# Seven-product down units: one VectorE take replaced by a ScalarE copy and an accumulating DMA, and a one-column sigmoid behind the samples' softmax

## The chip, the cores and the metric

The kernel runs on one core of a Trainium2 chip. The metric is device time in microseconds (us) of one execution, the median of several runs. The engines are TensorE (PE; its weight loads are PEld), VectorE (DVE), ScalarE (ACT), GpSimd (POOL) and SyncE (SP); each works through its own queue in order, and semaphores order them against each other. SP issues the loads of weights, POOL the accumulating DMAs.

## The reference

One inference step of a hybrid encoder trunk of two layers (model width 1024). It works on 640 frames at once: 512 of a new stream and 16 each of eight running streams. Each layer is, cut to its core:

```
x += 0.5 * swiglu(rmsnorm(x, norm_ffn1), w_ffn1_gu, w_ffn1_down)      # "a0", "a1"
z  = rmsnorm(x, norm_mix) @ w_in            # conv B, C, V | q, k, v | gates
y_c = B * causal_depthwise_conv3(C * V)
y_a = chunk_band_attention(q, k, v, rel_bias)   # 8 heads x 64
m  = sigmoid(g_c) * (y_c @ w_conv_out) + sigmoid(g_a) * (y_a @ w_attn_out)
x += m @ w_o
x += 0.5 * swiglu(rmsnorm(x, norm_ffn2), w_ffn2_gu, w_ffn2_down)      # "b0", "b1"

def swiglu(h, w_gu, w_down):                # w_gu: 1024 x 5632, w_down: 2816 x 1024
    g, u = split(h @ w_gu, 2)
    return (silu(g) * u) @ w_down
```

A final RMSNorm follows. New keys, values and conv rows are outputs too. All data are float32.

## The kernel before

**Layout.** `x` is held transposed in SBUF: `xall` has 128 partitions, 8 rows of the model width and 640 columns, the frames. `t1` and `t2` are the columns 0 to 319 and 320 to 639. Each product is done in three matmuls of float32r, with both operands split into a high and a low part (`whi`, `wlo` for weights): high by high, low by high, high by low. ScalarE makes the high parts with a copy (`ACT.copy`, L307 for weights), VectorE the low parts with a subtraction (L312).

**Seven products for eight.** Most of the big products treat their operands as 2 x 2 blocks and use a scheme of seven block products in place of eight. The operand combinations are named X11, X21, XN6, XT5, XT7, X22 and XT4; the weights of one unit are four slabs, each a sum or a plain piece. One PSUM bank collects several of these products in turn, and in between it is read out, with what it holds at that moment: later products add to it.

**The feed-forward networks.** `ffn` goes over 22 units of 128 of the 2816 hidden channels, in chunks (`FFNS`): a0 4, 4, 4, 4, 4, 2; b0 2, 4, 4, 4, 8; a1 4, 4, 4, 4, 4, 2; b1 3, 4, 4, 4, 4, 3. `gate_up` does the gate and up products of one unit by seven. A chunk of four that is neither before the plain part nor the last is also multiplied with `w_down` by seven: `down_rows`, twice for each chunk (a first call for the rows of `x` 0 to 3, and a second, `second = True`, for 4 to 7), called during the next chunk behind its second and third `gate_up` units. That makes 4, 3, 5 and 4 chunks in a0, b0, a1 and b1. The last chunk goes into `x` by plain products and takes the next norm's inputs with it (`nxt.final`).

**One `down_rows` call.** Banks A (two halves, tile names `daa`, `dab`) and B (`dba`, `dbb`) and two single banks `c` (`dca`, `dcb`) are filled by TensorE in this order, twelve matmuls each (L960): X11 into A, X21 into B, XN6 on top of A, XT5 into `c`, XT7 on top of A, X22 on top of `c`, XT4 on top of A. What a bank holds after a step goes into `x` in one of two ways. `take` (L989) is one VectorE instruction that reads the bank and adds it, scaled, to the rows of `x`. `stage` (L974, L977) is a ScalarE copy of the bank into an SBUF tile of the tag `cap`, which has five buffers in turn, and `send` (L984) an accumulating DMA from there into `x`, issued by POOL. `c1_` (A after X11), `u2_` (A after XN6) and `c5_` (`c` after XT5) go by stage and send; B, `c` after X22, and A after XT7 and after XT4 by take. The next product that adds to a bank must wait until it has been read.

`gate_up` uses the same `cap` buffers: one for `c1_`/`u2` (named `both` in the code) and one for `c5_`.

**Order.** Under `manual_schedule` the named engines work in the order of the program. In the first two units that feed a chunk by seven this holds for TensorE, VectorE and ScalarE; after that (`free`) only TensorE's order is fixed, and a scheduler sets the others', up to the last chunk.

**The mixer.** `attention` fixes only TensorE's order. It does the prompt's attention and then that of the eight samples: `sscores(b)` (scores and `softmax`, whose exponential is L1604 and reciprocal L1607) and `svalues(b)`. Between them the stream `others` runs, whose last piece is the first pair of gates, `gate_pair(0)`, with the layer's first two sigmoids (L1125). Then comes `outputs`, in program order on three engines: its first `gate_pair` (banks `qa`, `qb`, `qc`) copies the bank `qa` with ScalarE at L1277 after X11 and at L1287 after XN6. ScalarE evaluates a function from a table of its set; going to a function of another set takes an ACT_TABLE_LOAD. The tile `early` (one column) is written by activations that serve only to bring a table in.

Of the kernel before, what the change touches and what calls it, by code (L numbers as in the profile page):

```python
# [12 lines left out]
AF = mybir.ActivationFunctionType  # L13
# [7 lines left out]
NB = 8  # L21
# [10 lines left out]
FT = FF // P  # L32
# [150 lines left out]
def trunk(ctx: ExitStack, tc: tile.TileContext, xin, wst, small, pbias, samplebias, kcache, vcache,  # L183
# [44 lines left out]
    for kind, inside in kinds():  # L228
        n = len(fourth)
# [118 lines left out]
    class Tiles:  # L348
# [6 lines left out]
        def take(self):  # L355
            if self.at == self.n:
                self.cur, (kind, _, width) = slab(hold[0])
                assert kind == "plain"
                self.at, self.n = 0, width // P
            j = self.at  # L360
            self.at += 1
            return tuple(c[:, j * P : (j + 1) * P] for c in self.cur)
# [578 lines left out]
                next(p.work)  # L941
                p.done += 1

    def down_rows(fp, n, ms, pairs, tails, later):


        A, B = (acc(f"d{i}{n}") for i in "ab")
        a, b = ([z[:, u, :HT] for u in range(2)] for z in (A, B))
        c = [att(f"dc{n}_{u}")[:, :HT] for u in range(2)]
        t1, t2 = slice(0, HT), slice(HT, T)  # L950
        second = ms[0] > 0

        def mul(ps, s, half, kind, start):
            for u in range(2):
                for i, pair in enumerate(pairs):
                    kp = half * NP + 2 * u + i
                    wh, wl = (z[:, kp * P : (kp + 1) * P] for z in s)
                    xh, xl = pair.X[kind]
                    for j, (w, y) in enumerate(((wh, xh), (wh, xl), (wl, xh))):
                        PE.matmul(ps[u], w, y, start=start and i == 0 and j == 0,  # L960
                                  stop=i == 1 and j == 2, skip_group_check=True)

        def place(name):
            step(later, f"r{int(second)}{name}")

        def tail():
            for t in tails:
                t(False)
            tails.clear()

        def stage(name, ps, scale=0.5):
            z = fp.tile([P, 2, HT], F32, tag="cap", name=f"{name}{n}", bufs=5)
            if ps is A:
                ACT.activation(z, two(A), AF.Copy, scale=scale)  # L974
            else:
                for u in range(2):
                    ACT.activation(z[:, u], ps[u], AF.Copy, scale=scale)  # L977
            return z

        def rows(r, cols):  # L980
            return xall[:, ms[r] : ms[r] + 3 : 2, cols]

        def send(z, r, cols):
            POOL.dma_start(rows(r, cols), z, accum_op=ALU.add)  # L984

        def take(ps, r, cols, scale=0.5):
            xs = rows(r, cols)
            for d, z in ((xs, two(ps)),) if ps in (A, B) else zip((xs[:, 0], xs[:, 1]), ps):
                DVE.scalar_tensor_tensor(out=d, in0=z, scalar=scale, in1=d, op0=ALU.mult, op1=ALU.add)  # L989

        s0 = quiet()
        mul(a, s0, 0, X11, True)
        c1 = stage("c1_", A)
        prep(used[0] + 1)
        begin()
        if not second:
            tail()
        flush()
        place("d1")
        mul(b, s0, 1, X21, True)  # L1000
        take(B, 0, t1)
        send(c1, 0, t1)
        s1 = slab(True)[0]
        flush()
        mul(a, s1, 0, XN6, False)
        u2 = stage("u2_", A)
        mul(c, s1, 1, XT5, True)
        c5 = stage("c5_", c, -0.5)
        s2 = slab(True)[0]
        if second:  # L1010
            tail()
        mul(a, s2, 0, XT7, False)
        take(A, 1, t2, -0.5)
        send(c5, 1, t2)
        flush()
        ahead()
        mul(c, s2, 1, X22, False)
        take(c, 0, t2)
        send(u2, 0, t2)
        s3 = slab(True)[0]  # L1020
        ahead()
        mul(a, s3, 0, XT4, False)
        take(A, 1, t1, -0.5)
        flush()

    def ffn(name, fp, ex, goff, after, end=False):


        act, tails, later, pairs = {}, [], [], {}
        first_two = FFNS[name][0][-1] == 4  # L1030
        nxt = None
        chunks, plain = FFNS[name]
        last = FT - chunks[-1]
        hold[0] = True

        mode = ExitStack()
        free = min(j for j in range(FT) if by_seven(name, j)) + 2

        def order(engines):
            mode.close()  # L1040
            mode.enter_context(tc.manual_schedule(engines=engines))

        order(ORDERED)
        if plain:
            ex = opening(fp, name, goff, plain, act.__setitem__, tails)
        for what, a in ffn_order(name):
            if what == "gu" and a == free:
                order({mybir.EngineType.PE})
            if what == "cut":
                order(ORDERED)  # L1050
            if what in ("std", "cut"):
                continue
            if what == "gu":
                pair = None
                if by_seven(name, a):
                    i, odd = divmod(a - chunk_at(name, a)[0], 2)
                    if not odd:
                        at = chunk_at(name, a)[0]
                        rows = at and by_seven(name, at - 1)
                        pairs[a] = Pair(fp, f"{name}_{a}", i, later, TURNS[i if rows else i + 2])  # L1060
                    pair = pairs[a - odd]
                gate_up(fp, f"{name}_{a}", ex, a == plain, tails, act.__setitem__, a, pair, later,
                        a - chunk_at(name, a)[0])
                continue
            if what == "rows":
                ms, js = a
                down_rows(fp, f"{name}_{js[0]}_{ms[0]}", ms, [pairs[j] for j in js[::2]], tails, later)
                continue
            js = a[0][1]
            if js[0] == last or len(a) * len(js) >= KT:  # L1070
                for t in tails:
                    t()()
                tails.clear()
            if after is not None and js[0] == last:
                nxt = nxt or after()
            if end and js[0] == last:
                nxt.all([act[j] for j in js])
                break
            for m, js in a:
                if js[0] == last and m < 2 and first_two:  # L1080

                    if m == 0:
                        two_pd = [acc(f"pd{name}_{js[0]}_{i}") for i in range(2)]
                        ws = [[tiles.take() for _ in js] for i in range(2)]
                        for ks in (js[:-1], js[-1:]):
                            for p, w in zip(two_pd, ws):
                                for j in ks:
                                    multiply(p, w[j - js[0]], act[j], j == js[0], j == js[-1])
                    pd = two_pd[m]
                else:  # L1090
                    pd = acc(f"pd{name}_{js[0]}_{m}")
                    product(pd, [act[j] for j in js])
                done = nxt and m == KT - 1
                if nxt:
                    nxt.weights(m)
                DVE.scalar_tensor_tensor(out=halves(x[m]), in0=two(pd), scalar=0.5,
                                         in1=halves(x[m]), op0=ALU.mult, op1=ALU.add)
                if not done:
                    flush()
                if nxt:  # L1100
                    nxt.final(m)
        hold[0] = False
        if not nxt:
            flush()
        mode.close()
        return nxt
# [240 lines left out]
    def attention(l, h, norms, stats, ops, mp, yas, ycp, both, others):  # L1347
# [170 lines left out]
        def sscores(b):  # L1518
# [22 lines left out]
            with soon():  # L1541
                DVE.tensor_tensor_reduce(out=s, in0=pss, in1=sbias, scale=1.0, scalar=NEG,
                                         op0=ALU.add, op1=ALU.max, accum_out=st[:, 0, 0:1])

                softmax(s, st, [(0, KS)])
            held[b] = box, st, vraw, vn

        def svalues(b):
# [48 lines left out]
    def softmax(s, st, parts):  # L1597


        n = len(parts)  # L1600
        with soon():
            DVE.tensor_scalar(out=st[:, 1, :n], in0=st[:, 0, :n], scalar1=-1.0, scalar2=None, op0=ALU.mult)
        for i, (o, w) in enumerate(parts):
            ACT.activation(s[:, o : o + w], s[:, o : o + w], AF.Exp, bias=st[:, 1, i : i + 1],  # L1604
                           accum_out=st[:, 2, i : i + 1])
        with soon():
            DVE.reciprocal(st[:, 3, :n], st[:, 2, :n])  # L1607
# [286 lines left out]
```

## Time and profile before

| | |
|---|---|
| time, median of 3 runs | 2521.71 us (2521.63 to 2521.96) |
| time of the profiled execution | 2522.08 us |
| its span, first to last instruction | 2520.3 us |
| TensorE busy | 2501.4 us |
| VectorE busy | 2118.3 us |
| ScalarE busy | 1325.6 us |
| POOL busy | 185.4 us |
| takes in `down_rows`, L989, 128x640 from bank A | 64, 0.82 us each |
| accumulating DMAs, L984 | 96 of 320 KB each |

In the rows of the profile, L12 is line 12 of the kernel; a name such as `daa` or `c_a` is the program's name of a tile without its numbers, the tile written stands before the arrow and those read behind it. "idle before ... <-" names what ended an engine's wait. Rows in the order of time begin with the start and the duration in us. A matmul's duration reaches into the next one's, so the distance of starts tells TensorE's pace.

### The profile page before, as it was taken

Reading aid. Unit: us, or ns where it says so; the run is one execution under the profiler, and the core shown is the slowest. Engines: PE = TensorE matmul, PEld = TensorE weight load, DVE = VectorE, ACT = ScalarE, POOL = GpSimd, SP = SyncE. Lnnn points to the kernel's source line nnn. Section 1 sums busy time; section 2 is a strip of 40 time slices with the busy share of each in tenths; the row PEclk is TensorE's granted clock in tenths of the full one; section 3 lists DMA queues with packets and bytes.
Section 4 is the critical chain, followed back from the end, with each engine's and each line's share of the span. In section 5 each row is a group of like instructions: output and inputs, shape, how many; then the busy total and the mean of one; then the engine's idle time right before and its main releaser. Section 6 shows DMA issues by size and latency. Waiting matters only on the chain.

```text
span 2520.3 us, 42929 instructions
## 1 busy us (share of the span) xinstructions
PE 2501.4 (99%) x17192; PEld 2440.7 (97%) x17192; DVE 2118.3 (84%) x3347; ACT 1325.6 (53%) x2084; POOL 185.4 (7%) x249
## 2 busy tenths in 40 slices
PE   9999999999999999999999999999999999999998
PEld 8999999888999999999999999998889999999998
DVE  7889888878677899988699999888786768899997
ACT  7445556664444545555455555557644455455553
POOL 0000112111000001000001000021110000010000
PEclk9999999999999999999999999999999999999999
DMA  4233444334222234343224343443342222243434
GB/s 144 76 104 104 115 115 126 107 113 163 76 84 93 76 101 115 105 111 100 84 76 113 111 116 100 115 118 124 130 138 84 76 93 76 86 114 109 123 100 99
DMA packets 99320, 265.40 MB, mean 105 GB/s; under 512 B 9680, under 2 KB 45136, under 8 KB 99120
## 3 DMA queue, kind: packets, MB, share of 16 engines
q1 hardware_dynamic: 69408, 220.76, 26.7%
q0 software_dynamic: 28992, 41.26, 9.3%
q8 instruction: 135, 2.21, 0.4%
q10 hardware_dynamic: 720, 0.65, 0.1%
q14 instruction: 65, 0.53, 0.1%
HBM read 222.70 MB, written 7.94 MB: 92 GB/s over the span
## 4 chain that ended last, share of the span: by engine, by line
PE 92%; DVE 4%; ACT 3%; issue 1%; DMA 0%; SPq 0%; DVEq 0%; ACTq 0%
PE pab L397 12%; PE paa L397 11%; PE pcb L397 6%; PE pca L397 5%; PE daa L960 5%; PE py L374 4%; PE po L374 4%; PE qa L397 4%; PE pdb L374 4%; PE dab L960 4%; PE pbb L397 3%; PE pba L397 3%; PE pda L374 2%; PE pv L1400 2%; PE ma_cv L397 2%; PE poa L374 2%
## 5 line engine op out<-in xcount | busy, mean ns | idle before, releaser
L312 DVE TENSOR_TENSOR wlo<-raw,whi 128x1024 fp32r<-128x1024 f32 (+1 forms) x566 | 586.4, 1039 | 177.7 <-ACT whi L307 173.3
L307 ACT CAST whi<-raw 128x1024 fp32r<-128x1024 f32 (+1 forms) x566 | 509.1, 903 | 371.4 <-PE pbb L397 38.7
L307 ACT CAST whi<-s 128x1024 fp32r<-128x1024 f32 (+1 forms) x152 | 144.4, 950 | 272.3 <-issue 89.2
L397 PE MATMUL pab<-xhib,whi 128*128 128x320 f32 x704 | 218.0, 310 | 0.0
L397 PE MATMUL pab<-xhib,wlo 128*128 128x320 f32 x704 | 217.6, 309 | 0.0
L397 PE MATMUL pab<-xlob,whi 128*128 128x320 f32 x704 | 217.4, 309 | 0.0
L397 PE MATMUL paa<-xhia,wlo 128*128 128x320 f32 x640 | 197.7, 309 | 0.7 <-DVE wlo L312 0.7
L397 PE MATMUL paa<-xhia,whi 128*128 128x320 f32 x640 | 197.9, 309 | 0.0
L397 PE MATMUL paa<-xloa,whi 128*128 128x320 f32 x640 | 197.5, 309 | 0.0
L312 DVE TENSOR_TENSOR wlo<-s,whi 128x1024 fp32r<-128x1024 f32 (+1 forms) x152 | 166.5, 1096 | 9.8 <-ACT whi L307 9.8
L397 PEld LDWEIGHTS pab<-xhib,wlo 128*128 128x128 f32 x704 | 132.1, 188 | 0.3
L397 PEld LDWEIGHTS pab<-xhib,whi 128*128 128x128 f32 x704 | 132.2, 188 | 0.2
L397 PEld LDWEIGHTS pab<-xlob,whi 128*128 128x128 f32 x704 | 132.2, 188 | 0.2
L397 PEld LDWEIGHTS paa<-xhia,wlo 128*128 128x128 f32 x640 | 120.1, 188 | 1.3 <-DVE wlo L312 1.3
L397 PEld LDWEIGHTS paa<-xhia,whi 128*128 128x128 f32 x640 | 120.1, 188 | 0.1
L397 PEld LDWEIGHTS paa<-xloa,whi 128*128 128x128 f32 x640 | 120.1, 188 | 0.1
L984 POOL DMA_DIRECT2D x<-c_b x28 | 33.8, 1208 | 1105.2 <-ACT c_b L977 457.5
L397 PE MATMUL pcb<-xhib,wlo 128*128 128x320 f32 x352 | 108.9, 309 | 0.0
L397 PE MATMUL pcb<-xhib,whi 128*128 128x320 f32 x352 | 108.7, 309 | 0.0
L397 PE MATMUL pcb<-xlob,whi 128*128 128x320 f32 x352 | 108.7, 309 | 0.0
L984 POOL DMA_DIRECT2D x<-c_a x36 | 43.6, 1211 | 865.0 <-ACT whi L307 386.2
L251 DVE TENSOR_TENSOR raw<-raw,raw 128x512 f32<-128x512 f32 x152 | 103.9, 684 | 1.1 <-DMA raw<-in_wst 0.5
(681 smaller groups left out, 7945.5 us busy)
## 6 DMA issues: line engine op xcount, KB each, us to landing
raw<-in_wst SPq DMA_DIRECT2D x378, 512.0 KB, 3.5
x<-c_a POOLq DMA_DIRECT2D x36, 320.0 KB, 4.1
x<-c_b POOLq DMA_DIRECT2D x28, 320.0 KB, 4.1
kc<-in_kcache SPq DMA_DIRECT2D x32, 256.0 KB, 3.9
vc<-in_vcache SPq DMA_DIRECT2D x16, 512.0 KB, 4.5
x<-u_a POOLq DMA_DIRECT2D x18, 320.0 KB, 5.4
x<-u_b POOLq DMA_DIRECT2D x14, 320.0 KB, 5.5
bias<-in_pbias POOLq DMA_DIRECT2D x16, 256.0 KB, 3.7
```

Of the source, the lines that this page charges most:

```text
L251: DVE.tensor_tensor(out=out, in0=a, in1=b, op=ALU.add)
L307: ACT.copy(hi[:, d], src[:, c])
L312: DVE.tensor_tensor(out=lo, in0=src, in1=hi.bitcast(F32), op=ALU.subtract)
L374: PE.matmul(ps[:, a, :HT], w, x[:, a * HT : (a + 1) * HT], start=first and j == 0, stop=last and j == 2)
L397: PE.matmul(ps, a, b, start=start and kp == 0 and j == 0, stop=stop and kp == NP - 1 and j == 2, skip_group_check=True)
L960: PE.matmul(ps[u], w, y, start=start and i == 0 and j == 0, stop=i == 1 and j == 2, skip_group_check=True)
L984: POOL.dma_start(rows(r, cols), z, accum_op=ALU.add)
L1400: PE.matmul(pv[t], xx[:, t * P : (t + 1) * P], w[:, kk * AW : (kk + 1) * AW], start=c == 0 and kk == 0 and j == 0, stop=c == KT // 2 - 1 a ...
```

## The change

`down_rows` gets a flag `border`. It is true for the last chunk by seven of a network if the chunk behind it has fewer than four units, which is so in a0, a1 and b1 and not in b0; 3 of 16 chunks, so 6 of 32 calls. Where it is false, A after XT7 no longer goes into `x` by the VectorE take: ScalarE copies it, scaled by -0.5, into a new `cap` tile `c7_`, and POOL adds it to the rows of `x` by DMA, ahead of the DMA of `c5_` into the same place. In the mixer, the last `sscores` gets a sigmoid of one column into `early`, which reads what the softmax's reciprocal wrote.

```
-    def down_rows(fp, n, ms, pairs, tails, later):
+    def down_rows(fp, n, ms, pairs, tails, later, border):
...
         mul(a, s2, 0, XT7, False)
-        take(A, 1, t2, -0.5)
+        if border:
+            take(A, 1, t2, -0.5)
+        else:
+            send(stage("c7_", A, -0.5), 1, t2)
         send(c5, 1, t2)
...
-                down_rows(fp, f"{name}_{js[0]}_{ms[0]}", ms, [pairs[j] for j in js[::2]], tails, later)
+                down_rows(fp, f"{name}_{js[0]}_{ms[0]}", ms, [pairs[j] for j in js[::2]], tails, later,
+                          js[-1] + 1 == last and FT - last < 4)
...
                 softmax(s, st, [(0, KS)])
+                if b == NB - 1:
+                    ACT.activation(early, st[:, 3, 0:1], AF.Sigmoid)
             held[b] = box, st, vraw, vn
```

## The prediction

> **What bounds the kernel now.** I read the page first: the busy shares and the chain of work that ended last.
>
> ```profile
> span 2520.3 us, 42929 instructions
> PE 2501.4 (99%) x17192; PEld 2440.7 (97%) x17192; DVE 2118.3 (84%) x3347; ACT 1325.6 (53%) x2084; POOL 185.4 (7%) x249
> PE 92%; DVE 4%; ACT 3%; issue 1%; DMA 0%; SPq 0%; DVEq 0%; ACTq 0%
> ```
>
> TensorE is busy for 2501.4 of 2520.3 us. The change alters none of its instructions, so it can only win back, or add to, the moments in which TensorE waits. VectorE's 84% is no bound by itself, and lightening it brings nothing except where VectorE is what TensorE waits for. So the second view is the list of waits, by the weight loads that precede each matmul (what waited, for whom, us in total, times, longest):
>
> ```profile
> PEld daa L960 <- DVE x L989: 2.8, 7, 0.4
> PEld dab L960 <- DVE x L989: 2.4, 6, 0.4
> PEld qa L397 <- ACT capsm L1287: 1.3, 2, 0.6
> ```
>
> Two of the entries belong to the places that the diff touches. Thirteen times a `down_rows` call waits 0.4 us (5.2 in all) for a VectorE take (L989), and twice the gate products of the mixer wait 0.6 us for a ScalarE copy. Thirteen is a number that the code knows: of the 16 chunks done by seven (4, 3, 5 and 4 in a0, b0, a1 and b1) three are the border chunks that keep the take, one each in a0, a1 and b1; 3 + 4 = 7 are left in the two a's (`daa`) and 3 + 3 = 6 in the two b's (`dab`). Each has two calls, so 26 calls change, and one of the two waits in each chunk. The third view, the order of time, shows which one. This is a second call (`ms[0] > 0`) of a0, TensorE's rows first:
>
> ```profile
> 202.57 0.31 PE L960 MATMUL daa<-thia,wlo 128*128 128x320 f32 x1
> ...
> 204.18 0.31 PE L960 MATMUL dca<-aloa,whi 128*128 128x320 f32 x1
> 204.33 0.31 PE L960 MATMUL dca<-ahia,wlo 128*128 128x320 f32 x1
> 204.77 0.42 PE L960 MATMUL daa<-t4hia,whi 128*128 128x320 f32 x1
> 205.03 0.31 PE L960 MATMUL daa<-t4loa,whi 128*128 128x320 f32 x1
> ```
>
> Matmuls start 0.15 us apart (204.18 to 204.33). The XT7 block ends with the one that starts at 202.57 and runs 0.31, at 202.88. Twelve matmuls into `c` follow, and XT4 adds to bank A again, due at 204.33 + 0.15 = 204.48. It starts at 204.77, and the next start comes 0.26 after instead of 0.15. The call loses (0.44 - 0.15) + (0.26 - 0.15) = 0.40 us; 13 x 0.40 = 5.2, the sum of the wait rows. What XT4 waits for is the reading of A, on VectorE:
>
> ```profile
> 202.76 1.23 DVE L312 TENSOR_TENSOR wlo<-raw,whi 128x1024 fp32r<-128x1024 f32 x1 [0.45 <-ACT whi L307]
> 203.90 0.82 DVE L989 SCALAR_TENSOR_TENSOR x<-daa,x 128x640 f32<-128x640 f32 x1
> ```
>
> The take could start at 202.88, but a weight subtraction of 1.23 us is ahead of it; it ends at 204.72, and XT4 starts 0.05 later. In a first call the take is in time:
>
> ```profile
> 178.63 0.82 DVE L989 SCALAR_TENSOR_TENSOR x<-daa,x 128x640 f32<-128x640 f32 x1
> 179.83 0.31 PE L960 MATMUL daa<-t4hia,whi 128*128 128x320 f32 x1
> ```
>
> It ends at 179.45, 0.38 before XT4 starts.
>
> **The third block on ScalarE.** What ScalarE does around the late call, and the time that a copy of the same size out of the same bank takes there (min/median/max ns):
>
> ```profile
> 202.62 0.73 ACT L924 CAST thia<-doa 128x640 fp32r<-128x640 f32 x1
> 204.58 1.05 ACT L307 CAST whi<-s 128x1024 fp32r<-128x1024 f32 x1 [1.24 <-PE dca L960]
> L974 ACT ACTIVATE c_a<-daa x18: 680/707/709, 171.2 to 1653.6; 128x640 f32<-128x640 f32 x18
> ```
>
> ScalarE's cast ends at 203.35, and then it stands idle for 1.24 us until the next cast may start. The new copy `c7_` fits there: 203.35 + 0.71 = 204.06, against 204.48 for XT4. If the scheduler puts it ahead of the cast, it ends at 202.88 + 0.71 = 203.6. Either way 0.4 us is to spare, so the wait goes: bounds 0 and 0.40 a call, and I take 0.40, since nothing else stands in that gap. Below nothing is not expected from this copy unless it ends after 204.72, another 0.66 us late. In first calls ScalarE has finished its last copy before the block ends and has no more than the next weight cast behind it:
>
> ```profile
> 177.36 0.43 ACT L977 ACTIVATE c_a<-dca 128x320 f32<-128x320 f32 x1
> 179.94 1.05 ACT L307 CAST whi<-s 128x1024 fp32r<-128x1024 f32 x1 [2.15 <-PE dca L960]
> ```
>
> The gap from 177.79 to 179.94 takes the 0.71 us, so nothing is lost, and nothing is won where nothing waited. VectorE loses 26 x 0.82 = 21 us and ScalarE gains 26 x 0.71 = 18 us of busy time; neither is at its limit in these calls, so I cost both at nothing beyond the 5.2 us. If the cover on ScalarE were gone, the price would be the lateness itself.
>
> **The added DMA, and the wait that comes with it.** `c7_` and `c5_` now both add into the same rows and columns of `x`, so the DMA of `c5_` must wait until that of `c7_` has landed, where it waited for the take before. POOL's queue holds it in order, with `u2_` behind:
>
> ```profile
> 205.31 1.20 POOL L984 DMA_DIRECT2D x<-c_a  x1 [4.72 <-DVE x L989]
> 206.04 1.70 POOL L984 DMA_DIRECT2D x<-u_a  x1
> DMA to landing us min/median/max: 4.1/5.0/7.5
> ```
>
> From the end of the XT7 block: the copy ends after 1.2, the first DMA lands after 1.2 + 5.0 = 6.2, POOL takes 1.2 for the second, and `u2_` lands at 6.2 + 1.2 + 5.0 = 12.4; with the longest landings, at 1.2 + 7.5 + 1.2 + 7.5 = 17.4. Nobody else uses POOL in this phase. Who waits is the owner of the staging buffer. The five `cap` buffers go round; with four stages in a call and two in a gate-up unit, the buffer of `u2_` comes back at `c1_` of the next call, or after a second call at the first copy of the gate-up unit after next:
>
> ```profile
> 195.88 0.71 ACT L974 ACTIVATE c_a<-daa 128x640 f32<-128x640 f32 x1
> 220.93 0.43 ACT L820 COPY c_a<-paa 128x320 f32<-128x320 f32 x1
> ```
>
> The first call's XT7 block ends 1.6 before the 179.83 above, at 178.23, so its buffer has 195.88 - 178.23 = 17.65 us; the second call's has 220.93 - 202.88 = 18.05 us. Both are more than 17.4, so I cost the queue at nothing. [...]
>
> **The early sigmoid.** The mixer's first sigmoid brings a table load, and behind it ScalarE works without a pause up to the copy for which TensorE waits:
>
> ```profile
> 643.40 1.28 ACT L1125 ACT_TABLE_LOAD   x1
> 644.70 0.83 ACT L1125 ACTIVATE g<-g,sm 128x640 f32<-128x640 f32 x1
> 645.56 0.37 ACT L1579 COPY ya<-ptx 64x256 f32<-64x256 f32 x1
> 645.95 0.83 ACT L1125 ACTIVATE g<-g,sm 128x640 f32<-128x640 f32 x1
> 646.81 0.43 ACT L1277 COPY capsm<-qa 128x320 f32<-128x320 f32 x1
> ...
> 651.11 0.42 ACT L1287 COPY capsm<-qa 128x320 f32<-128x320 f32 x1
> 645.61 0.31 PE L397 MATMUL qa<-hhim,wlo 128*128 128x320 f32 x1
> ...
> 650.89 0.31 PE L397 MATMUL qc<-hhim,wlo 128*128 128x320 f32 x1
> 651.58 0.41 PE L397 MATMUL qa<-thi,whi 128*128 128x320 f32 x1 [0.38 <-ACT capsm L1287]
> 651.83 0.30 PE L397 MATMUL qa<-tlo,whi 128*128 128x320 f32 x1
> ```
>
> TensorE loses (0.69 - 0.15) + (0.25 - 0.15) = 0.64 us here, and the same in layer 1: 1.3 us. Without the load of 1.28 us the copy of 646.81 can begin when its matmuls end, 645.61 + 0.31 = 645.92, 0.89 earlier, and the copy of 651.11 with it, at 650.22 to 650.64. It is needed at 650.89 + 0.15 = 651.04, so the whole 0.64 goes. The load now sits behind the last softmax:
>
> ```profile
> 627.34 0.62 ACT L307 CAST whi<-raw 128x512 fp32r<-128x512 f32 x1
> 629.05 0.37 ACT L1559 COPY ss<-sptp 128x256 f32<-128x256 f32 x1 [1.09 <-PE sptp L1557]
> 631.58 0.42 PE L1567 MATMUL spy<-vn,ss 16*32 16x128 f32 x8
> L601 ACT ACTIVATE early<-epst x4: 202/203/203, 37.3 to 2106.2; 128x1 f32<-128x1 f32 x4
> ```
>
> From 627.96 it needs 1.28 + 0.20 us, up to 629.44; the next copy comes 0.39 late and ends at 629.81, 1.8 us before its reader at 631.58. So the addition costs nothing. [...]
>
> **Sum.** 13 x 0.40 + 2 x 0.64 = 6.5 us. The profiled execution took 2522.08 (span 2520.3), so 2515.6; the median of the runs, 2521.71, is 0.4 below it, so 2515.2 us, 0.26% faster.
>
> **Rivals.** *The copy comes late on ScalarE.* If the scheduler sets one more cast of 0.73 us ahead of it, it ends at 203.35 + 0.73 + 0.71 = 204.79, where the take ends at 204.72 now; nothing of the 0.40 us is won, and the sigmoid's 1.3 us are left: 2520.4. For it: outside the first units of a network only TensorE's order is fixed. Against it: in the gap of 1.24 us nothing else was ready. *The sigmoid's gain goes elsewhere.* Another wait (a weight cast, the transfer of a raw tile) holds the chain from 645.92 on; 5.2 us are left: 2516.5. *The queue becomes the wait*, the rival on the slower side. Its place is the reuse of `u2_`'s buffer: 1.2 + 1.2 + two landings exceed 17.65 from 7.6 us a landing, just above the longest of 7.5. At 9.0 us ScalarE's copy comes 2.75 late. That copy starts at 195.88, right behind its block, and ends at 196.59; its bank is needed when 12 further matmuls (12 x 0.15 = 1.8 us) have run, at some 197.6, a cover of 1.0. Some 1.7 us of each of 26 calls would show, 44 us: 2515 + 44 = 2559. For it: more transfers share the engines. Against it: the median landing is 5.0, and it leaves 5 us. *The change doesn't do what it says* (the waits simply pass to another reader of bank A): no change, 2521.7; it would need the second copy or take of that bank to be late too, and no row shows one.
>
> **How the numbers follow.** A measurement of this kernel tells about 0.2%, 5 us, from no change, so faster means below 2516.7. Forecast 0.68; sigmoid without effect 0.11 (at 2516.5, on the edge); late copy 0.08; no change 0.04; queue or another slower outcome 0.09. Faster: the forecast and a part of the second, less some of the forecast's upper end: 0.70. Same: the rest, the late copy and no change: 0.21. Slower 0.09. The range reaches from 2514.2 (1 us for waits behind VectorE elsewhere that shrink too) to 2518.0 (half of the 5.2 us stays): the forecast, the second case and the first part of the late copy, 0.8 of the chance.
>
> **What would show it.** In the changed profile: no row of `daa` or `dab` waiting for `x` at L989 but for the border chunks; 26 new copies of about 0.71 us on ScalarE, ending some 1.2 us after the XT7 block; VectorE's busy time down by about 21 us; POOL's DMA of `c5_` waiting 4 to 8 us for a landing, with no idle ScalarE behind it; the table load near 628 and 1875 us, and `qa` without its wait of 0.6. The prediction is wrong if new waits of `daa`/`dab` for ScalarE appear, if `c1_` copies wait for a DMA, or if the weight loads wait for `whi` or `wlo` in these calls.

## The result, and the profile after

The changed kernel takes 2515.6 us (median of 10 runs, 2514.72 to 2516.51), the kernel before in the same comparison 2522.06 (10 runs, 2521.63 to 2523.09): ratio 0.9974, with a 95% interval of 0.9966 to 0.9983. That is 6.5 us, as forecast (2515.2 us). The profiled execution took 2514.72 us. Its page, busy shares and the chain of work that ended last:

```profile
span 2512.7 us, 42964 instructions
PE 2496.8 (99%) x17192; PEld 2440.6 (97%) x17192; DVE 2101.2 (84%) x3321; ACT 1342.7 (53%) x2112; POOL 216.3 (9%) x275
PE 95%; DVE 3%; ACT 2%; issue 0%; DMA 0%; DVEq 0%; ACTq 0%
```

TensorE does the same 17192 matmuls in a span 7.6 us shorter, and the chain runs over TensorE for 95% of it instead of 92%. In the list of waits, the rows of `daa`, `dab` and `qa` are gone, and no wait of more than 0.3 us has come in their place. What is left was there before, such as the wait at the kernel's start (`poa`, 5.9 us before) and the two behind a weight subtraction in `paa`:

```profile
PEld poa L374 <- ACT whi L620: 5.6, 1, 5.6
PEld paa L397 <- DVE wlo L312: 1.3, 2, 0.7
```

The same second call of a0 in the order of time (each row begins with start and duration):

```profile
202.28 0.31 PE L960 MATMUL daa<-thia,wlo 128*128 128x320 f32 x1
204.04 0.31 PE L960 MATMUL dca<-ahia,wlo 128*128 128x320 f32 x1
204.18 0.31 PE L960 MATMUL daa<-t4hia,whi 128*128 128x320 f32 x1
204.34 0.31 PE L960 MATMUL daa<-t4loa,whi 128*128 128x320 f32 x1
...
202.33 0.72 ACT L924 CAST thia<-doa 128x640 fp32r<-128x640 f32 x1
202.96 0.71 ACT L974 ACTIVATE c_a<-daa 128x640 f32<-128x640 f32 x1
...
202.47 1.23 DVE L312 TENSOR_TENSOR wlo<-raw,whi 128x1024 fp32r<-128x1024 f32 x1 [0.45 <-ACT whi L307]
```

XT7's last matmul ends at 202.28 + 0.31 = 202.59. VectorE is at its weight subtraction until 203.70, as before. ScalarE ends its cast and copies the bank from 202.96 to 203.67, and XT4 starts at 204.18, 0.14 behind the matmul ahead of it and 0.16 ahead of the next: no pause. Compared start by start, all 13 places take 0.40 us less than before (0.30 at XT4's first matmul and 0.10 at the one behind it), 5.3 in all, and the two places of `qa` 0.64 and 0.63 less. The remaining 1.0 us of the 7.6 lies at the kernel's start (0.3), at its last matmuls (0.3) and in differences too small to name.

POOL in that call, and the landings of these DMAs:

```profile
204.03 1.19 POOL L984 DMA_DIRECT2D x<-c_a  x1 [3.75 <-ACT c_a L974]
205.46 1.19 POOL L984 DMA_DIRECT2D x<-u_a  x1 [0.24 <-issue]
208.95 1.22 POOL L984 DMA_DIRECT2D x<-c_a  x1 [2.31 <-DVE t4loa L909]
DMA to landing us min/median/max: 4.1/4.9/8.3
```

The first is `c7_`, the last `c5_`, 4.9 us later. `u2_` stands between them: the scheduler put it ahead of the one that has to wait for a landing. The sigmoid, on ScalarE:

```profile
625.53 0.62 ACT L307 CAST whi<-raw 128x512 fp32r<-128x512 f32 x1
626.17 1.28 ACT L1551 ACT_TABLE_LOAD   x1
627.46 0.20 ACT L1551 ACTIVATE early<-sst 128x1 f32<-128x1 f32 x1
627.57 0.36 ACT L1565 COPY ss<-sptp 128x256 f32<-128x256 f32 x1
...
641.69 0.83 ACT L1129 ACTIVATE g<-g,sm 128x640 f32<-128x640 f32 x1
...
648.45 0.42 ACT L1291 COPY capsm<-qa 128x320 f32<-128x320 f32 x1
```

The load is at 626.17, the gates' sigmoid follows without one, and the copy of `qa` that was late no longer shows as a wait. Before and after, the trace has 16 loads of 1.28 us: one at the kernel's start, one at the first square root and 14 where one of square root, SiLU, exponential and sigmoid follows another; copies and squares stand between them without one.

### The profile page after: what moved, and what is told of

It is laid out like the page before. It is cut to its first block, busy times and chain, and to the rows that moved or that the text cites. A ratio compares the mean times of both kernels' runs of the same rounds, so it can differ in the third digit from the quotient of the medians.

```text
span 2512.7 us, 42964 instructions
## 1 busy us (share of the span) xinstructions
PE 2496.8 (99%) x17192; PEld 2440.6 (97%) x17192; DVE 2101.2 (84%) x3321; ACT 1342.7 (53%) x2112; POOL 216.3 (9%) x275
## 4 chain that ended last, share of the span: by engine, by line
PE 95%; DVE 3%; ACT 2%; issue 0%; DMA 0%; DVEq 0%; ACTq 0%
PE pab L397 12%; PE paa L397 11%; PE pcb L397 6%; PE pca L397 5%; PE daa L960 5%; PE py L374 4%; PE po L374 4%; PE qa L397 4%; PE dab L960 4%; PE pdb L374 4%; PE pbb L397 3%; PE pba L397 3%; PE dca L960 3%; PE poa L374 2%; PE pda L374 2%; PE pv L1404 2%
## 5 line engine op out<-in xcount | busy, mean ns | idle before, releaser
L984 POOL DMA_DIRECT2D x<-c_b x40 | 48.3, 1207 | 1083.8 <-ACT whi L307 475.6
L984 POOL DMA_DIRECT2D x<-c_a x50 | 60.6, 1214 | 837.4 <-ACT whi L307 402.8
```

## The experiments

Each was run beside the kernel before, which took 2521.78 us in the first group of four, 2521.76 in the second and 2522.19 in the third. Line numbers shift by a few between the kernels.

**Theory:** what is won is TensorE's 13 + 2 waits, because the bank is read in time. **Rivals:** it is the relief of VectorE at large; or the added DMAs cost something that hides in the sum.

**The two parts alone.** `rows_only` leaves out the sigmoid, `sigmoid_only` leaves `down_rows` as it was.

```
                 softmax(s, st, [(0, KS)])
-                if b == NB - 1:
-                    ACT.activation(early, st[:, 3, 0:1], AF.Sigmoid)
```

> The change without its sigmoid. Theory A (bank release: the change wins because in 13 second calls bank A is read before XT4 needs it): 13 x 0.40 = 5.3 us below the kernel before, some 2516.8 us, and the gate products keep their two waits of 0.64 us for the ScalarE copy. Rival (the two parts share one cause, the order that the scheduler chose anew): the gain is not 5.3, and the gates' wait changes though the sigmoid is not there.

> The sigmoid alone, with all takes on VectorE. Theory: 2 x 0.64 = 1.3 us below the kernel before, some 2520.8 us; the 13 waits for the take at 0.40 us stay. Rival (another wait holds that chain): no difference, 2522.1 us.

`rows_only`: 2517.05 us (2515.93 to 2518.19), ratio 0.9981 [0.9972, 0.9990]; `sigmoid_only`: 2520.48 (2520.28 to 2521.0), ratio 0.9995 [0.9986, 1.0004]. The list of waits of `rows_only` keeps

```profile
PEld qa L397 <- ACT capsm L1291: 1.3, 2, 0.6
```

and that of `sigmoid_only`

```profile
PEld daa L960 <- DVE x L989: 2.8, 7, 0.4
PEld dab L960 <- DVE x L989: 2.4, 6, 0.4
```

Each part takes away its own rows and only those: 4.7 and 1.3 us. The intervals reach some 0.1% (2 us) to either side, and that of `sigmoid_only` contains 1.0000; differences of 1 to 2 us rest here on the rows of the traces and on times that do not overlap (2521.0 at most against 2521.3 at least), not on the interval. The first is 0.5 short of 5.2 although all 13 places lose their 0.40 in its trace. The profiled execution of `rows_only`, its slowest, lost time elsewhere, at the start of the kernel (window, length, busy time and count for PE, PEld, DVE, ACT and POOL, then PEclk, the granted TensorE clock as a share of full speed, DMA share, GB/s):

```profile
5.00:17.00 12.00, 11.09 (x48) 10.16 (x49) 9.32 (x13) 9.75 (x15) 0.00 (x0) 1.00 0.99 367
```

48 matmuls there, where the kernel before has 57 and the changed one 59, for more of them start 0.27 us apart instead of 0.15 (20 starts, against 15 and 18), with more pauses of 0.43 to 0.65 us between them. The PEclk of 1.00 says nothing here: the trace's clock record begins only at 13.85 us in this run, at 10.55 in the kernel before and at 11.08 in the changed one. The 9 to 11 that are missing are worth 1.3 to 1.6 us at 0.147 each (from 60 to 400 us the changed kernel does 2319 matmuls in 340 us). The change does nothing there. That such starts also put the median of `rows_only` 0.5 us off is likely but not shown, since its other executions have no trace.

**The same bank, read in time by VectorE.** `take_first` is the kernel before with one order changed: in second calls the take stands ahead of the next unit's weight subtraction (whose work waits in the list `pending`).

```
         if second:
+            kept = list(pending)
+            pending.clear()
             tail()
+            order({mybir.EngineType.PE, mybir.EngineType.DVE})
         mul(a, s2, 0, XT7, False)
         take(A, 1, t2, -0.5)
         send(c5, 1, t2)
+        if second:
+            pending.extend(kept)
         flush()
+        if second:
+            order({mybir.EngineType.PE})
```

> The kernel before, with one swap on VectorE in each second call: the take of bank A after XT7 comes ahead of the weight subtraction of the next unit, which stood before it. No ScalarE copy, no added DMA, no sigmoid, the same work on every engine. Theory A (bank release): the take starts when the block ends, 0.8 us later bank A is free, 0.8 us before XT4; all 14 waits go (the border call of b1 too): 14 x 0.40 = 5.6 us, some 2516.5 us. Theory B (relief: what counts is that VectorE has 21 us less to do): nothing is won, 2522.1 us, since VectorE has the same work; or the subtraction, 0.8 us later, makes the next unit's weights late.

2516.70 us (2515.99 to 2517.92), ratio 0.9980 [0.9971, 0.9989]: 5.1 us faster with VectorE's work unchanged. Its page and the call:

```profile
PE 2498.2 (99%) x17192; PEld 2439.8 (97%) x17192; DVE 2116.4 (84%) x3347; ACT 1326.1 (53%) x2084; POOL 184.9 (7%) x249
```

```profile
203.06 0.82 DVE L989 SCALAR_TENSOR_TENSOR x<-daa,x 128x640 f32<-128x640 f32 x1 [0.61 <-PE daa L960]
203.81 1.22 DVE L312 TENSOR_TENSOR wlo<-raw,whi 128x1024 fp32r<-128x1024 f32 x1
204.48 0.31 PE L960 MATMUL dca<-ahia,wlo 128*128 128x320 f32 x1
204.62 0.31 PE L960 MATMUL daa<-t4hia,whi 128*128 128x320 f32 x1
204.78 0.31 PE L960 MATMUL daa<-t4loa,whi 128*128 128x320 f32 x1
```

The take ends at 203.88, and XT4 follows without a pause. The subtraction starts 0.9 us later, counted from the end of the XT7 block (203.81 against 203.03, where it was 202.76 against 202.88), and nobody waits for it. One new wait is in its list, in a0's last chunk: TensorE waits for a take, and that take for the landing of `u2_`'s DMA:

```profile
PEld pda L374 <- DVE x L1103: 0.7, 1, 0.7
DVE x L1103 <- DMA x<-u_a: 0.9, 1, 0.9
```

(The text on record counts 14 waits; there are 13. In b1's border chunk, two other matmuls stand between `c` and XT4, so that its take is in time.) So the 5 us are the order of two VectorE instructions, and a VectorE that is less busy is worth nothing beside it that these runs can tell.

**The copy without the DMA.** `stage_add` copies with ScalarE as the change does, but VectorE adds the copy to `x`.

```
-            send(stage("c7_", A, -0.5), 1, t2)
+            add(rows(1, t2), rows(1, t2), stage("c7_", A, -0.5))
```

> The change without its sigmoid and without its DMA: ScalarE copies bank A into the staging tile, and VectorE adds the tile to x from SBUF. VectorE keeps as many instructions as before. Theory A (bank release): the same 5.3 us as with the DMA, some 2516.8 us. Theory B (relief of VectorE): little or nothing is won, about 2522 us. Theory C (the added DMA gives part of the gain back through POOL and the DMA engines): faster than the change without its sigmoid, by more than 1 us.

2516.45 us (2515.81 to 2517.53), ratio 0.9979 [0.9970, 0.9988], without the sigmoid; VectorE is as busy as before the change:

```profile
PE 2497.7 (99%) x17192; PEld 2441.0 (97%) x17192; DVE 2118.1 (84%) x3347; ACT 1342.7 (53%) x2110; POOL 185.7 (7%) x249
```

It is level with `rows_only` (0.6 us apart, where each run's times spread over 1.7 to 2.3 us): the copy is what frees the bank, and by which way the copy gets into `x` makes no difference that these runs can tell.

**Which calls matter.** `second_only` keeps the copy and DMA in second calls alone (with the sigmoid), `first_only` in first calls alone (without it).

```
-        if border:
+        if border or not second:      # second_only
+        if border or second:          # first_only
             take(A, 1, t2, -0.5)
```

> The changed kernel, with copy and DMA in the 13 second calls alone; the 13 first calls have their VectorE take again. The sigmoid stays. Theory A (bank release in second calls): the same time as the changed kernel, some 2515.6 us, with 13 DMAs less. Theory B (relief of VectorE): half of the 5.3 us is gone, some 2518.2 us.

> Copy and DMA in the 13 first calls alone, the second calls as before, no sigmoid. Theory A: no difference to the kernel before, 2522.1 us, since no first call waited; 13 added DMAs and 13 added ScalarE copies cost nothing. Theory B (relief of VectorE): half the gain, some 2519.5 us. Theory C (the added transfers cost): slower than before by what they cost.

`second_only`: 2515.19 us (2514.77 to 2515.59), ratio 0.9974 [0.9964, 0.9984], with 13 copies and 13 DMAs fewer than the change. `first_only`: 2523.74 (2523.09 to 2525.61), ratio 1.0009 [1.0000, 1.0018], 2.0 us slower (its fastest time lies above the slowest of the kernel before, 2522.48). The waits of `first_only`:

```profile
PEld daa L960 <- DVE x L989: 2.8, 7, 0.4
PEld dab L960 <- DVE x L989: 2.4, 6, 0.4
PEld pda L374 <- DVE x L1100: 2.4, 1, 2.4
ACT ya L438 <- DMA x<-u_a: 3.0, 1, 3.0
```

The 13 waits stay, as they should. The new pair of waits has nothing to do with bank A. In a0's last chunk, ScalarE's first write of the mixer's tile `ya` waits 3.0 us for the landing of a DMA out of a staging buffer. The norm's next `hhim` stands behind it on ScalarE; `hlom`, which needs `hhim`, and behind it the takes of `pda` wait on VectorE, and TensorE waits for those.

**Where a landing costs.** The next two kernels meet the same place. `all_calls` drops the border exception; `cap4` is the changed kernel with four staging buffers for five.

```
-        if border:
-            take(A, 1, t2, -0.5)
-        else:
-            send(stage("c7_", A, -0.5), 1, t2)
+        send(stage("c7_", A, -0.5), 1, t2)          # all_calls
...
-            z = fp.tile([P, 2, HT], F32, tag="cap", name=f"{name}{n}", bufs=5)
+            z = fp.tile([P, 2, HT], F32, tag="cap", name=f"{name}{n}", bufs=4)   # cap4, all tiles of the tag
```

> The changed kernel without its exception: the six border calls too go by copy and DMA. Theory A: one more wait of 0.40 us goes (b1's border call), some 2515.2 us, if the two landings in a row, about 11.4 us after the XT7 block, are in time for the last chunk's update of those rows of x, which by the pace of TensorE comes some 13 us after the block. Rival (the landing is what the border spares): VectorE's last updates of x wait for the DMA of c5 in a0, a1 and b1, and the time goes up by 1 us or more at each.

> The changed kernel with four staging buffers in place of five. The next owner of the buffer of u2 is then the gate-up unit right behind, which writes it some 10.4 us after the XT7 block; in the changed kernel's profile u2's DMA is issued 2.9 us after the block and should land some 5 us later, at 7.9. Theory (the queue on POOL is hidden with room to spare): no difference, some 2515.6 us. Rival (the queue is next in line): ScalarE's copy in those units waits for a landing, and with landings of up to 7.5 us part of the 26 places loses 1 us or more: above 2520 us.

`all_calls`: 2522.62 us (2521.92 to 2523.39), ratio 1.0003 [0.9994, 1.0012]: 7.0 more than the changed kernel, and so all that the change wins. `cap4`: 2517.88 (2517.03 to 2520.77), ratio 0.9986 [0.9977, 0.9995]: 2.3 more. The waits of `all_calls` and its rows in a0's last chunk:

```profile
ACT ya L438 <- DMA x<-c_a: 5.7, 1, 5.7
PEld pda L374 <- DVE x L1097: 5.0, 1, 5.0
```

```profile
418.62 0.84 ACT L432 ACTIVATE hhim<-x,sm 128x640 fp32r<-128x640 f32 x1 [1.72 <-DVE x L1097]
419.48 1.21 POOL L984 DMA_DIRECT2D x<-c_a  x1 [3.14 <-DMA x<-c_a]
425.13 0.74 ACT L438 ACTIVATE ya<-x 128x640 f32<-128x640 f32 x1 [5.68 <-DMA x<-c_a]
429.49 0.90 PE L374 MATMUL pda<-ahia,whi 128*128 128x320 f32 x2 [4.73 <-DVE x L1097]
430.19 0.73 PE L374 MATMUL pda<-aloa,whi 128*128 128x320 f32 x2
430.72 0.73 PE L374 MATMUL pda<-ahia,wlo 128*128 128x320 f32 x2
```

The same two instructions of ScalarE in the changed kernel:

```profile
418.34 0.83 ACT L432 ACTIVATE hhim<-x,sm 128x640 fp32r<-128x640 f32 x1 [1.70 <-DVE x L1100]
419.08 0.73 ACT L438 ACTIVATE ya<-x 128x640 f32<-128x640 f32 x1
```

`c5_`'s DMA has to wait for `c7_`'s landing, is issued at 419.48, and `ya` starts at 425.13, when it has landed. TensorE waits 5.0 us, and then two matmuls take 0.53 (430.19 to 430.72): 0.27 each, not 0.147, for some 16 of them, another 2 us. The granted clock (the first number behind the counts, 0.55) shows it, in `all_calls`:

```profile
430.00:434.00 4.00, 4.00 (x18) 4.00 (x17) 3.00 (x5) 3.61 (x7) 0.00 (x0) 0.55 0.21 59
```

It is 1.00 in the changed kernel from 424 to 430. `cap4` waits less, and for `u2_`:

```profile
ACT ya L438 <- DMA x<-u_a: 2.7, 1, 2.7
PEld pda L374 <- DVE x L1100: 2.0, 1, 2.0
```

No copy in a `gate_up` unit or a `down_rows` call waits for a buffer, although there are only four.

Whether `ya` waits depends on which transfer it has to wait for, and that differs from kernel to kernel. By the semaphores in the traces, the last one is that of `c1_` of a0's last call in the kernel before and in the changed one, that of `c5_` in `second_only` and `all_calls`, and that of `u2_` in `first_only` and `cap4`. In the changed kernel, too, `u2_` lands late: it is issued at 414.96 and lands 7.2 us later, 3.1 us after `ya` has started at 419.08, and nobody waits for it. In layer 1 of `all_calls`, `c5_` lands 6.1 us after `ya` has started, again without a wait.

**The landing taken out.** Three kernels repeat these with one or two pieces of a0's last call added by VectorE in place of DMA: `u2_` in `first_only_noland` and `cap4_noland`, `c5_` and `u2_` in `all_calls_noland`.

```
+        def give(z, r, cols):
+            if second and n.startswith("a0_16"):
+                add(rows(r, cols), rows(r, cols), z)
+            else:
+                send(z, r, cols)
...
-        send(u2, 0, t2)
+        give(u2, 0, t2)
```

> The kernel with copy and DMA in the 13 first calls alone and no sigmoid, but with u2 of a0's last call added to x by VectorE instead of by DMA. Theory (its 2 us over the kernel before are the one wait of ya for u2's landing, not the 13 added DMAs): the time of the kernel before, some 2521.8 us, and the 13 waits for the take stay. Rival (the added transfers cost): it stays at some 2523.7 us.

> The changed kernel with four staging buffers, with u2 of a0's last call added to x by VectorE instead of by DMA. Theory (four buffers are enough for the rows, and the 2.3 us that they cost were the one wait of ya for u2's landing): some 2515.4 us. Rival (the copies in the gate-up units wait for landings): it stays above 2517 us.

> The kernel with copy and DMA in all 32 calls, but in the last call of a0 (second = True) the blocks c5 and u2 are added to x by VectorE from the staging tile instead of by DMA. Theory (in the run with all calls the first write of the mixer's tile ya waited 5.7 us on ScalarE for the landing of c5, whose staging buffer lies under that tile, and TensorE's plain products waited 5.0 us behind it; border calls otherwise only win): the wait of ya for a DMA is gone, and the time falls by some 7 us to the changed kernel's or 0.4 below, 2515.0 to 2515.6 us. Rival (the late landing makes the updates of x in the last chunks late, in b1 too): above 2517 us.

`first_only_noland`: 2521.77 us (2521.52 to 2522.21), ratio 0.9998 [0.9989, 1.0007]; the wait is gone and with it the 2 us, so 13 added DMAs by themselves cost nothing. `cap4_noland`: 2515.61 (2515.36 to 2516.82), ratio 0.9973 [0.9962, 0.9984], level with the change: four buffers are enough, and `cap4`'s 2.3 us were that one wait. `all_calls_noland` missed: 2520.62 (2518.19 to 2521.36), ratio 0.9991 [0.9982, 1.0000], where 2515 was expected. Its rows tell why:

```profile
419.71 0.82 DVE L251 TENSOR_TENSOR x<-x,c_a 128x640 f32<-128x640 f32 x1 [2.56 <-DMA x<-c_a]
422.77 0.72 ACT L438 ACTIVATE ya<-x 128x640 f32<-128x640 f32 x1
```

`ya` no longer waits, but VectorE's add of `c5_` goes into the place into which `c7_` is being added, so it waits for that landing in `ya`'s stead, with VectorE's queue behind it, and TensorE waits 3.4 us. So this run does not show the landing taken out, only moved. What the border exception is worth, 7 us, more than the change wins in all, rests on `all_calls` and its trace: 5.0 us of waiting and 2 at the slow pace behind it.

**Both orders together.** `take_first_sig` is `take_first` with the sigmoid.

> The kernel before with the take of bank A ahead of the weight subtraction in the second calls, and with the early sigmoid: no added copy and no added DMA. Theory: the two gains add up, 14 x 0.40 + 2 x 0.64 = 6.9 us less any wait in a0's last chunk; 2515.2 us, level with the changed kernel. Rival (the order forced on VectorE costs in a0's last chunk, where the run without the sigmoid showed a wait of 0.6 us more): some 2516 us.

2516.08 us (2515.38 to 2517.32), ratio 0.9974 [0.9965, 0.9984]; the wait for a take in a0's last chunk, 0.8 us here (behind a wait of VectorE of 1.1 us for `u2_`'s landing), is what its trace has more than that of the change. The best version run is `second_only` at 2515.19. Its distance to the changed kernel, 0.4 us, is less than the scatter of either.

## Why the prediction was right

**The 13 waits.** Right in count, place and size: 13 times 0.40, 5.3 us measured for the 5.2 of the sum. The cause is shown: with the take in time (`take_first`) the same is won, with only the second calls changed (`second_only`) all of it, with only the first calls changed nothing of it.

**The copy on ScalarE.** Predicted to end 1.2 us after the block; 1.08 in the call shown (203.67 less 202.59). XT4 starts 1.6 after the block (204.18). The latest of the 26 copies ended 1.35 after its block. The rival of a second cast ahead of it did not occur.

**The sigmoid.** Right: 1.26 us of the 1.28. The load stands right behind a weight cast (0.02 us after its end) and right ahead of the copy of `sptp`, as placed, and no reader of either waits for it. The next activation starts 1.29 us behind the load's start (626.17 to 627.46), as in the rows from which the prediction worked (643.40 to 644.70, 1.30).

**VectorE and ScalarE.** ScalarE's 18 us are 17.1. VectorE's 21 are 17.1: the prediction multiplied rows, but they overlap (a row begins 0.09 before the end of the one ahead, 203.61 against 203.70, so that each row taken away shortens the busy time by less than its length). Nothing in the time hangs on it.

**The queue.** The step was wrong in its order and right in its price, at the last call partly by luck. The prediction queued `u2_` behind the waiting `c5_`; the program issues it ahead in all 26 calls, since only TensorE's order is fixed there. The rival priced from that, slower from 7.6 us a landing, had thus no ground: `c5_`, now the last, took 8.3 us to land in one call, and ScalarE waited for none of these DMAs. The luck is at the end of a0: `u2_` lands after `ya` has started, and only because `ya` does not wait for `u2_` in this kernel does that cost nothing; in `cap4`, where it does, 2.3 us are lost.

**The rival on the slower side** was looked for at the wrong place. The prediction followed the buffers round within the calls; what a late landing does cost lies behind the last call, where the memory is used for something else. The border flag, whose reason the prediction did not see, keeps the landing of `c5_` early (419.06, against 425.05 in `all_calls`). It is not the whole protection: `first_only` and `cap4` keep the flag and wait for `u2_`. That `ya` lies over a staging buffer is inferred: `hhim` reads the same row of `x` ahead of it without a wait, the DMAs of the last call add into rows 4 to 7 and `ya` reads row 0, the wait is always for a DMA out of a staging buffer, and without that DMA it is gone. That the turn of the buffers, which shifts with the number of staged pieces, sets which of them lies there fits this, and is inferred too. Where the tiles lie was not printed, and moving `ya` was not tried.

**The sum.** 6.5 us predicted; 7.4 between the two profiled executions and 6.5 between the medians. The 0.9 between them is the scatter of single executions.

## What to carry to other kernels

Where TensorE is busy 99% of the span, list its waits by place, count them against the code and price each from the distances of starts; the busy share of the other engines said nothing here. Before moving work to another engine to shorten a late read, see whether the instruction ahead of it could come after it: two VectorE instructions changed in order won what 26 copies and 26 DMAs won. An accumulating DMA that hides in the steady state can appear at the end of a phase, where (as inferred here) its buffer's memory goes to another tile; follow the last one of each phase to its landing, and do so again after any change to the number of buffers or of pieces in them.

## What was not expected of the hardware

A wait of TensorE can cost more than its length: 5.0 us in `all_calls` were followed by some 16 matmuls at 0.27 us (granted clock 0.55), 3.4 us in `all_calls_noland` by some 13, and 2.0 us in `cap4` by 13 (granted clock 0.50), while 2.4 us in `first_only` were followed by none (1.00). The changes of the granted clock fit steps of 3.413 us: from the start of its record it stays at 1.00 for 2501.97 us in the kernel before and for 2495.14 us in the changed one, 733 and 731 times 3.4133, and is 0.50 from there to the kernel's end. The halved stretches behind two of the waits last one and two of these: 3.41 us in `cap4`, and an estimated 6.8 us in `all_calls` (0.73 on average from 424 to 430 and 0.55 from 430 to 434, so halved for 3.2 and 3.6 us). In these traces the wait of 2.0 us differs from that of 2.4 in its place, counted on in steps of 3.413 us. In `cap4` the whole wait lies in one step (first row), and the clock is halved in the next (second row); in `first_only` the boundary, counted to 426.14, cuts the wait in two (last two rows), and the clock stays at 1.00:

```profile
424.52:427.93 3.41, 1.62 (x11) 1.36 (x10) 3.06 (x4) 3.41 (x6) 0.29 (x2) 1.00 0.25 100
427.93:431.34 3.41, 3.41 (x15) 3.41 (x14) 2.89 (x5) 3.41 (x7) 0.00 (x0) 0.50 0.17 32
422.72:426.14 3.42, 3.00 (x21) 2.74 (x19) 1.08 (x2) 2.69 (x5) 0.29 (x2) 1.00 0.87 328
426.14:429.55 3.41, 1.73 (x12) 1.73 (x13) 3.41 (x6) 3.41 (x6) 0.00 (x0) 1.00 0.00 0
```

TensorE is busy for 1.62 us of the step that is followed by a halved clock, and for 3.00 and 1.73 us of the two that are not. That the place decides is inferred from these two waits, out of four in all; no run moved a wait to test it. The number of slow matmuls at the kernel's start varies too: 20 starts of 0.27 us in `rows_only` against the 15 and 18 above.
